# Plain fp32 matmuls on unsplit operands for the projections of one of three mixers in an encoder trunk

## The chip, the core and the metric

The kernel runs on one core of one Trainium2 chip. The metric is the device time of the program in microseconds; lower is better. A core has five engines that run side by side and meet at semaphores: PE (TensorE, the matrix multiplier; its weight loads are shown apart as PEld), DVE (VectorE), ACT (ScalarE), POOL (GpSimd) and SP (SyncE, which here issues every DMA).

## The reference

Two layers, each with an RMSNorm, one wide input projection, three mixers side by side (A: HGRN2, B: retention, C: RWKV-7), a gated merge, and an output projection. The sequence has 256 tokens, the model 1024 features. Cut to what matters:

```python
for l in range(DEPTH):                                # DEPTH = 2
    h = rmsnorm(x, norm_g[l])                         # 256 x 1024, float32
    proj = h @ w_in[l]                                # 1024 x 18688
    (a_q, a_ff, a_fb, a_i, a_g, b_q, b_k, b_v, b_g, c_s, c_g, merge) = split(proj)
    y_a = hgrn2_mixer(a_q, a_ff, a_fb, a_i, ...) * silu(a_g)
    y_b = retention_mixer(b_q, b_k, b_v, ...) * silu(b_g)
    y_c = rwkv7_mixer(c_s, ...) * silu(c_g)           # c_s: r, k, v and the codes of decay and a
    gates = sigmoid(merge)
    mixed = gates_0 * (y_a @ w_a) + gates_1 * (y_b @ w_b) + gates_2 * (y_c @ w_c)
    x = x + mixed @ w_out[l]
return rmsnorm(x, final_norm_g)
```

All of it is float32.

## The kernel before

**Weights.** The weights of a layer lie in 93 blocks of 1024 rows and 256 columns, each stored as two halves of 512 KB (`_blocks`). 17 of them feed mixer C: `codes`, and for each of eight pairs of heads `("rk", p)` (128 columns of r and 128 of k) and `("vg", p)` (128 of v and 128 of the gate). 20 feed A, 24 feed B, 12 the merge gates, 16 the branch outputs and 4 the output.

**Split products.** Every block goes through `load_w`: a half is loaded into `wr` (line 182, on SP), ACT rounds it to float32r in `wh` (line 184), and DVE subtracts the two into `wl` (line 187). The tiles `wr`, `wh` and `wl` are each taken in turn from three buffers (`RW`, through `ring`). The norm writes its transposed output h in the same way, as `h_hi` (line 253, ACT) and `h_lo` (line 254, DVE), out of the PSUM tile `n_t`. `feat_mm` then issues three float32r matmuls for each k-tile of 128 rows, wh·h_hi, wh·h_lo and wl·h_hi, 128 x 128 by 256 columns, all summed in PSUM: 24 for a half, 48 for a block (line 200; line 210 in `tok_mm`, where h is the stationary side). `proj` joins load and matmuls, and gives a PSUM tile `pj` out of two taken in turn; the profile calls it by the block's key, `p_codes`, `p_rk`, `p_vg` and so on.

**Order.** A layer first runs `c_codes`. The loop over p from -2 to 7 then runs `c_scan` of pair p, `c_prep` and `c_solve` of pair p + 2, and one pair of heads of A (p = -1 to 2) or B (p = 3 to 6) as `FILL` has it. `c_prep` projects rk and vg, shifts them along the tokens (`shift`, lines 288 to 291), and makes the chunk products (lines 393 to 399). `c_solve` sends blocks of `c_Z` to DRAM and back as `c_M` (lines 410 and 414) and inverts small triangles on DVE (lines 425 to 444). The merge (`tail`) comes after the loop. This is the order of the program; the framework orders each engine's queue itself, by a planner that runs a model of the timeline (`schedule_with_timeline_sim`), so that in the trace the matmuls of several blocks are interleaved. Each queue runs in its order, and all loads and the solve's DMAs stand in the one queue of SP.

**Plain fp32.** The small matmuls of the mixers (lines 337, 393 to 395, 486 to 534, 712, 718 and others) take float32 tiles as they are. One such matmul leaves two records in the trace.

Of the kernel before, what the change touches and what calls it, by code (L numbers as in the profile page):

```python
# [8 lines left out]
F32 = mybir.dt.float32  # L9
# [8 lines left out]
T = 256  # L18
# [9 lines left out]
RW = (3, 3, 3)  # L28
# [4 lines left out]
# columns of a layer's packed parameters  # L33
# [9 lines left out]
# columns of the shape constants  # L43
# [9 lines left out]
# of the masks that A takes, and of the rotation that B takes  # L53
# [4 lines left out]
# blocks of weights in a layer, in the order of _blocks()  # L58
BK = {}


def _blocks():
    """(key, matrix, row range start, list of (column start, width)) of each block of 1024 rows and 256 columns."""
    r = [("codes", "w_in", 0, [(11264 + 3072, 256)])]
    for p in range(8):
        r.append((("rk", p), "w_in", 0, [(11264 + 128 * p, 128), (11264 + 1024 + 128 * p, 128)]))
        r.append((("vg", p), "w_in", 0, [(11264 + 2048 + 128 * p, 128), (14592 + 128 * p, 128)]))
    for p in range(4):
        for n, o in (("aff", 1024), ("afb", 2048), ("aq", 0), ("ai", 3072), ("ag", 4096)):
            r.append(((n, p), "w_in", 0, [(o + 256 * p, 256)]))  # L70
    for p in range(4):
        r.append((("bq", p), "w_in", 0, [(5120 + 256 * p, 256)]))
        r.append((("bk", p), "w_in", 0, [(6144 + 256 * p, 256)]))
        for h in (2 * p, 2 * p + 1):
            r.append((("bv", h), "w_in", 0, [(7168 + 256 * h, 256)]))
            r.append((("bg", h), "w_in", 0, [(9216 + 256 * h, 256)]))
    for m in range(3):
        for b in range(4):
            c = 256 * b
            r.append((("mg", m, b), "w_in", 0, [(15616 + 1024 * m + c, 256)]))  # L80
            for n, w, r0 in ((("wa", "w_branch_a", 0),), (("wb0", "w_branch_b", 0), ("wb1", "w_branch_b", 1024)),
                             (("wc", "w_branch_c", 0),))[m]:
                r.append(((n, b), w, r0, [(c, 256)]))
    for b in range(4):
        r.append((("wo", b), "w_out", 0, [(256 * b, 256)]))
    return r
# [8 lines left out]
def trunk(ctx: ExitStack, tc, x, wb, pp, lora, cst, gtab, ng, out, parts="ABCT", layers=L, dbg=None):  # L95
# [10 lines left out]
    # x and what its norm takes come before the other constants  # L106
# [27 lines left out]
    def ring(pool, shape, dt, tag, n, name):  # L134
        """a tile in the next of a tag's n buffers, in turn"""
        i = turn[tag] = (turn.get(tag, -1) + 1) % n
        return pool.tile(shape, dt, tag=f"{tag}{i}", bufs=1, name=name)

    h_hi = keep.tile([128, KT, T], F32R, name="h_hi")
    h_lo = keep.tile([128, KT, T], F32R, name="h_lo")  # L140

# [1 line left out]
    DP = []  # L143
    for l in range(L):
        d = keep.tile([128, 26 + 8 + 8 + 32], F32, name=f"dp{l}")
        p = P_[l]
        mu = p[:, PO["mu"]:PO["mu"] + 52]
        # 1 - mu0 - mu1
        V.tensor_add(d[:, 0:26], mu[:, 0:26], mu[:, 26:52])
        V.tensor_scalar(d[:, 0:26], d[:, 0:26], -1.0, 1.0, op0=ALU.mult, op1=ALU.add)  # L150
        V.tensor_scalar(d[:, 26:34], p[:, PO["kk"]:PO["kk"] + 8], -1.0, None, op0=ALU.mult)
        V.tensor_scalar(d[:, 34:42], p[:, PO["ka"]:PO["ka"] + 8], -1.0, 1.0, op0=ALU.mult, op1=ALU.add)
        V.tensor_scalar(d[:, 42:74], p[:, PO["w0"]:PO["w0"] + 32], -1.0, None, op0=ALU.mult)
        DP.append(d)

    # lower bounds: softmax over the layers with its maximum, cumulated, less the first
# [13 lines left out]
    # cumsum - p[0]  # L170
# [6 lines left out]
    def load_w(l, key):  # L177
        """the parts of a block's halves"""
        W = []
        for h in range(2):  # L180
            raw = ring(wp, [128, 1024], F32, "wr", RW[0], "wr")
            nc.sync.dma_start(raw, wb[2 * (l * NBLK + BK[key]) + h])
            hi = ring(wp, [128, 1024], F32R, "wh", RW[1], "wh")
            S.copy(hi, raw)  # L184
            lo = ring(wp, [128, 1024], F32R, "wl", RW[2], "wl")
            n = WS[h]
            V.tensor_sub(lo[:, 0:n], raw[:, 0:n], hi[:, 0:n].bitcast(F32))  # L187
            if n < 1024:
                G.tensor_sub(lo[:, n:], raw[:, n:], hi[:, n:].bitcast(F32))
            W.append((hi, lo))  # L190
        return W

    def feat_mm(o, W, f, h, first=True, last=True):
        """o[feature, t] (+)= W[:, f*128:+128]^T h; half f of the block holds these columns"""
        whi, wlo = (t.rearrange("p (k c) -> p k c", c=128) for t in W[f])
        hhi, hlo = h
        n = 0
        for k in range(KT):
            for a, b in ((whi, hhi), (whi, hlo), (wlo, hhi)):
                PE.matmul(o, a[:, k], b[:, k, :], start=(first and n == 0), stop=(last and n == 3 * KT - 1))  # L200
                n += 1

    def tok_mm(o, W, t, h):
        """o[t, column] = h[:, t-tile]^T W; a half of the block holds four k-tiles"""
# [14 lines left out]

    def sigmoid_of_exp(t):  # L220
        """t = exp(-x) -> sigmoid(x), in place; Ln ends at 2^64, where sigmoid(x) = 1 / t to the last bit"""
        V.tensor_scalar(t, t, EMAX, None, op0=ALU.min)
        S.activation(t, t, AF.Ln, bias=1.0)
        S.activation(t, t, AF.Exp, scale=-1.0)
# [5 lines left out]
    def silu_from(pool, src, shape, tag, tmp, bufs=1, tb=1):  # L230
        """silu of a projection in PSUM"""
# [8 lines left out]
    def norm_T(xs, ss, gb, pool):  # L240
        """xs and the sums of its squares by token; gb: the gains, on every partition"""
# [5 lines left out]
        for t in range(2):  # L247
            for j in range(0, KT, 4):
# [5 lines left out]
                V.tensor_sub(h_lo[:, j:j + 4, 128 * t:128 * t + 128], o, hi.bitcast(F32))  # L254

# [7 lines left out]
    # ================= C: RWKV-7 =================  # L263
    pers = {}

    def c_setup(pool):
        """tiles whose blocks off the diagonal stay zero"""
# [27 lines left out]
    def c_codes(l, pool):  # L295
        o = proj(l, "codes")
        cw = shift(l, o[:, 0], 24, pool, "c_cw")
        ca = shift(l, o[:, 1], 25, pool, "c_ca")
        # tanh(x) = 2 sigmoid(2 x) - 1
# [5 lines left out]
    def c_prep(l, p, codes, pool):  # L305
        """Everything of pair p up to the chunk products, evacuated and masked."""
# [6 lines left out]
        o1 = proj(l, ("rk", p))  # L313
        r = shift(l, o1[:, 0], p, pool, "c_r", 2)
        k = shift(l, o1[:, 1], 8 + p, pool, "c_k", 2)
        o2 = proj(l, ("vg", p))
# [3 lines left out]
        # normalised kk, negated  # L320
# [8 lines left out]
        # decay and a  # L329
# [21 lines left out]
        # its ninth block holds the stacked identity  # L351
# [4 lines left out]
        # bonus: sum of r k_d r_k over both directions  # L356
# [7 lines left out]
        # k~, beta~, alpha~, r~ of each direction, and the products within its chunks  # L364
# [6 lines left out]
        for d in range(2):  # L371
            # a chunk's blocks of 64: A_rk^T, r~, A_ak, A_rb^T, beta' (first alpha~), A_ab^T, k', diag g, alpha~^T
# [30 lines left out]
    def c_solve(l, p, st, pool):  # L403
        """Inverses of the diagonal 32 x 32 blocks of I - A_ab, one block and every fourth column a partition."""
# [17 lines left out]
        # inverses of the diagonal 4 x 4 blocks, in place: entry (i, k) of block I at 132 I + 32 k + i  # L422
# [8 lines left out]
        # this block's columns  # L431
        V.tensor_mul(tp, at(m, 0, (132, 8), (1, 4), (32, 4)), cc("hot")[:, None, None, :].to_broadcast([128, 8, 4, 4]))
        V.tensor_reduce(at(w, 0, (36, 8), (1, 4)), tp, axis=AX.X, op=ALU.add)
        # then four rows at a time
# [15 lines left out]
    def c_scan(l, p, st, pool, ydst):  # L450
# [10 lines left out]
        # v of each direction, transposed  # L461
# [18 lines left out]
        # (I - A_ab)^-1 [A_ak, alpha~^T] by blocks of 32, for a direction's four chunks at a time  # L480
# [14 lines left out]
        # what a chunk makes of its v and of the state before it: mt its output, mk the state after it  # L495
# [19 lines left out]
        # the state from chunk to chunk  # L515
# [24 lines left out]
        # group norm over a head's 64 partitions  # L540
# [14 lines left out]
    # ================= A: HGRN2 =================  # L555
    def a_pair(l, p, pool, ydst):
# [6 lines left out]
        # k = (1 - lb) sigmoid(-x), f = lb + (1 - lb) sigmoid(x); the first layer's lb is p[0] - p[0] = 0  # L563
# [28 lines left out]
    def a_head(l, hd, le, kq, v, g, pool, ydst):  # L592
        # decay sums within 128 positions: forward, and backward negated
# [10 lines left out]
        def pairs(e, s):  # L604
            """K (lower forward, upper backward) and Q (lower backward, upper forward), scaled"""
# [6 lines left out]
        # between the two tiles of 128  # L612
# [30 lines left out]
        # within 8 positions, from their middle  # L643
# [16 lines left out]
        # output, its norm over the 128 partitions and the gate  # L660
# [27 lines left out]
    # ================= B: retention =================  # L688
# [52 lines left out]
    # ================= merge and output =================  # L741
# [64 lines left out]
    # ================= layers =================  # L806
# [40 lines left out]
def _consts():  # L847
# [31 lines left out]
    # [head, j, j-tile * 256 + i]  # L879
# [7 lines left out]
def _pack(inputs):  # L887
# [4 lines left out]
    for l in range(L):  # L892
        for n, (key, mat, r0, cols) in enumerate(_blocks()):
            m = np.concatenate([a[mat][l, r0:r0 + 1024, c0:c0 + w] for c0, w in cols], 1)
            if key[0] in TOK:
                # halves of four k-tiles
                m = m.reshape(2, 4, 128, 256).transpose(0, 2, 1, 3)
            else:
                # halves of 128 columns
                m = m.reshape(8, 128, 2, 128).transpose(2, 1, 0, 3)  # L900
            wb[l * NBLK + n] = m.reshape(2, 128, 1024)

    def tiles(v):
        """a vector of n * 128 values as [128, n]"""
# [40 lines left out]
```

## Time and profile before

| what | value |
|---|---|
| device time, median of 3 runs | 1821.67 us (1819.37 to 1822.58) |
| profiled execution, first to last instruction (span) | 1821.9 us |
| mean granted clock of PE | 0.965 |
| instructions | 33791 |
| weights read, 372 halves | 512 KB each |
| HBM read | 229.22 MB |

The profile gives one execution of the program; of that execution it lists the span and no other time, and the span agrees with the median of the runs to 0.2 us. Its views are a page (busy time of each engine, 40 equal slices of the span, DMA queues, the chain of waits that ended last, the costliest groups of instructions) and answers about the trace: groups by line, instructions that touch a tile, waits, the chain in order of time, and busy time by windows.

How to read it: busy time of an engine says how much of a window it worked, not whether that work was waited for; the chain says what was waited for, at one moment after the other. PE's instructions overlap in the pipeline, so the pitch from start to start is the cost of a matmul in a row of matmuls, not its duration. The blocks of C are to be found by the tiles `p_codes`, `p_rk` and `p_vg`.

### The profile page before, as it was taken

What the parts mean: (1) busy time and instruction counts of PE and PEld (TensorE: products, weight loads), DVE (VectorE), ACT (ScalarE), POOL (GpSimd) and SP (SyncE); (2) the same over time, 40 slices, a digit from 0 to 9 for tenths busy, and PEclk for the clock granted to TensorE, in tenths of its full rate; (3) what the DMA queues carried; (4) which work ended last, traced back from release to release, by engine and by line L of the source; (5) the groups of instructions that cost most, each with busy time, mean ns of one, the idle gap of its engine ahead of it and who ended that gap; (6) DMA issues with size and microseconds to landing.
All of it is one profiled execution on the core that took longest, in us unless ns stands there. A gap on an engine that the chain in (4) does not pass through costs nothing.

```text
span 1821.9 us, 33791 instructions
## 1 busy us (share of the span) xinstructions
PE 1667.6 (92%) x12960; PEld 1625.0 (89%) x12960; DVE 1415.4 (78%) x2597; ACT 1056.5 (58%) x1940; POOL 322.0 (18%) x312
## 2 busy tenths in 40 slices
PE   6888899999999999999888789988999999999997
PEld 6877899898999998999888788988889999999997
DVE  5799898998878785565657989989998787846554
ACT  5665566757465545555556556757573656456453
POOL 1122222212120200010011222223131202100100
PEclk9989999999999999999988889999999999999999
DMA  6333223324344443755533233233244444437653
GB/s 221 116 118 105 79 96 102 117 86 138 119 155 141 146 148 133 244 200 187 198 114 118 99 100 91 88 109 107 93 133 125 144 142 154 142 131 245 208 186 116
DMA packets 127873, 250.30 MB, mean 137 GB/s; under 512 B 62304, under 2 KB 66784, under 8 KB 127456
## 3 DMA queue, kind: packets, MB, share of 16 engines
q1 hardware_dynamic: 127712, 248.15, 41.6%
q8 instruction: 102, 1.67, 0.4%
q14 instruction: 59, 0.48, 0.1%
HBM read 229.22 MB, written 14.68 MB: 134 GB/s over the span
## 4 chain that ended last, share of the span: by engine, by line
PE 49%; DVE 30%; issue 7%; DMA 6%; ACT 4%; SPq 2%; POOL 0%; DVEq 0%; ACTq 0%; POOLq 0%
PE t_o L200 10%; PE p_mg L200 8%; DVE wl L187 7%; DVE c_tq L439 3%; PE p_bv L210 3%; PE p_vg L200 3%; PE p_bg L200 2%; DMA c_M<-s 2%; PE pj L210 2%; PE c_p L393 2%; DMA s<-c_Z 2%; ACT wh L184 2%; DVE c_ts L441 2%; PE p_rk L200 1%; PE c_p L395 1%
## 5 line engine op out<-in xcount | busy, mean ns | idle before, releaser
L187 DVE TENSOR_TENSOR wl<-wr,wh 128x1024 fp32r<-128x1024 f32 x372 | 475.9, 1280 | 192.3 <-ACT wh L184 190.9
L184 ACT CAST wh<-wr 128x1024 fp32r<-128x1024 f32 x372 | 388.4, 1045 | 272.7 <-PE t_o L200 56.2
L200 PE MATMUL t_o<-yh,wh 128*128 128x256 f32 x512 | 144.7, 284 | 2.8 <-ACT yh L748 2.8
L200 PE MATMUL t_o<-yl,wh 128*128 128x256 f32 x512 | 145.0, 284 | 0.5 <-DVE yl L749 0.5
L200 PE MATMUL t_o<-yh,wl 128*128 128x256 f32 x512 | 144.6, 283 | 0.0
L608 POOL TENSOR_TENSOR a_sl<-a_kq,a_e 128x256 f32<-128x256 f32 x80 | 80.9, 1015 | 230.9 <-ACT a_e L618 66.0
L200 PE MATMUL p_mg<-h_hi,wh 128*128 128x256 f32 x384 | 109.6, 285 | 0.0
L200 PE MATMUL p_mg<-h_hi,wl 128*128 128x256 f32 x384 | 109.4, 285 | 0.0
L200 PE MATMUL p_mg<-h_lo,wh 128*128 128x256 f32 x384 | 108.7, 283 | 0.0
L200 PEld LDWEIGHTS t_o<-yh,wh 128*128 128x128 f32 x512 | 97.6, 191 | 3.2 <-ACT yh L748 3.2
L200 PEld LDWEIGHTS t_o<-yl,wh 128*128 128x128 f32 x512 | 97.9, 191 | 1.0 <-DVE yl L749 0.9
L200 PEld LDWEIGHTS t_o<-yh,wl 128*128 128x128 f32 x512 | 97.9, 191 | 0.0
L393 PE MATMUL c_p<-c_Z,bbd 128*128 128x192 f32 x256 | 68.9, 357 | 29.7 <-DVE bbd L388 25.0
L439 DVE TENSOR_TENSOR c_tq<-W,c_M 128x16 f32<-128x16 f32 (+6 forms) x112 | 89.0, 795 | 1.4
L200 PE MATMUL p_vg<-h_hi,wh 128*128 128x256 f32 x256 | 78.1, 305 | 8.1 <-ACT c_k L288 4.1
L399 ACT COPY c_Z<-c_p 128x192 f32<-128x192 f32 x128 | 40.3, 318 | 74.9 <-DVE c_Z L396 73.7
L200 PE MATMUL p_bg<-h_hi,wl 128*128 128x256 f32 x256 | 75.0, 293 | 4.6 <-DVE wl L187 4.6
L210 PE MATMUL p_bv<-wh,h_hi 128*128 128x256 f32 x256 | 76.1, 297 | 1.1 <-ACT b_z L694 1.1
L210 PE MATMUL p_bv<-wl,h_hi 128*128 128x256 f32 x256 | 75.4, 295 | 1.7 <-DVE wl L187 1.7
L200 PE MATMUL p_vg<-h_lo,wh 128*128 128x256 f32 x256 | 75.8, 296 | 0.0
L200 PE MATMUL p_vg<-h_hi,wl 128*128 128x256 f32 x256 | 75.6, 295 | 0.0
L210 PE MATMUL p_bv<-wh,h_lo 128*128 128x256 f32 x256 | 74.7, 292 | 0.0
(334 smaller groups left out, 5983.3 us busy)
## 6 DMA issues: line engine op xcount, KB each, us to landing
wr<-in_wb_dram SPq DMA_DIRECT2D x372, 512.0 KB, 3.3
c_M<-s SPq DMA_DIRECT2D x64, 128.0 KB, 2.7
c_lt<-in_lora_dram SPq DMA_DIRECT2D x16, 256.0 KB, 2.7
b_sw<-b_z SPq DMA_DIRECT2D x16, 256.0 KB, 3.9
b_gt<-in_gtab_dram SPq DMA_DIRECT2D x16, 256.0 KB, 3.4
yb<-b_y SPq DMA_DIRECT2D x16, 256.0 KB, 3.0
yr<-yb SPq DMA_DIRECT2D x8, 512.0 KB, 5.0
s<-c_Z SPq DMA_DIRECT2D x128, 16.0 KB, 1.9
```

What stands on the lines that cost most here:

```text
L184: S.copy(hi, raw)
L187: V.tensor_sub(lo[:, 0:n], raw[:, 0:n], hi[:, 0:n].bitcast(F32))
L200: PE.matmul(o, a[:, k], b[:, k, :], start=(first and n == 0), stop=(last and n == 3 * KT - 1))
L210: PE.matmul(o, a[:, k, t * 128:(t + 1) * 128], b, start=(n == 0), stop=(n == 3 * KT - 1))
L393: PE.matmul(o[:, 2:5], bbd[:, c], z[:, c, 1:8:3], start=True, stop=True)
L395: PE.matmul(o[:, 0:6:5], kbd[:, c], z[:, c, 1:8:6], start=True, stop=True)
L399: S.copy(z[:, c, 4:9:2], o[:, 4:7])
L439: V.tensor_mul(tp, W[:, 0:n, None, 0:j].to_broadcast([128, n, 4, j]), M[:, 0:j, j:j + 4].rearrange("p j i -> p i j")[:, None].to_broadcast ...
L441: V.tensor_reduce(sm, tp, axis=AX.X, op=ALU.add)
L608: G.tensor_mul(s5[:, :, :, 0], k5[:, 0:2, :, 0], e5[:, :, :, 0])
```

## The change

The 17 blocks of C are no longer split. A new function `proj_whole` loads each half into `wr` and issues one plain fp32 matmul for each k-tile, straight from `wr` and from `h_f`, a third copy of h in float32 that the norm writes on ACT from the same PSUM tile: 8 matmuls for a half, 16 for a block. `wr` has four buffers. `c_codes` and `c_prep` call `proj_whole`; A, B, the merge and the output keep the split products. The scratch space that is set aside for dynamic DMAs is cut to 1024 bytes. Comments are removed as well.

```diff
-RW = (3, 3, 3)
+RW = (4, 3, 3)
...
     h_lo = keep.tile([128, KT, T], F32R, name="h_lo")
+    h_f = keep.tile([128, KT, T], F32, name="h_f")
...
+    def proj_whole(l, key):
+
+        o = ring(ps, [128, 2, 256], F32, "pj", PB["pj"], f"p_{key if key == 'codes' else key[0]}")
+        for f in range(2):
+            raw = ring(wp, [128, 1024], F32, "wr", RW[0], "wr")
+            nc.sync.dma_start(raw, wb[2 * (l * NBLK + BK[key]) + f])
+            w = raw.rearrange("p (k c) -> p k c", c=128)
+            for k in range(KT):
+                PE.matmul(o[:, f], w[:, k], h_f[:, k], start=(k == 0), stop=(k == KT - 1))
+        return o
...
                 S.copy(hi, o)
                 V.tensor_sub(h_lo[:, j:j + 4, 128 * t:128 * t + 128], o, hi.bitcast(F32))
+                S.copy(h_f[:, j:j + 4, 128 * t:128 * t + 128], o)
...
     def c_codes(l, pool):
-        o = proj(l, "codes")
+        o = proj_whole(l, "codes")
...
-        o1 = proj(l, ("rk", p))
+        o1 = proj_whole(l, ("rk", p))
...
-        o2 = proj(l, ("vg", p))
+        o2 = proj_whole(l, ("vg", p))
...
-    nc = _bacc.Bacc("TRN2", target_bir_lowering=False, num_devices=1)
+    nc = _bacc.Bacc("TRN2", target_bir_lowering=False, num_devices=1, dynamic_dma_scratch_size=1024)
```

## The prediction

> **What bounds the kernel now.** I read the head of the page first, then a table of busy time by stretches, cut where the PSUM tiles of the projections first and last appear, then the chain of waits stretch by stretch.
>
> ```profile
> span 1821.9 us, 33791 instructions
> PE 1667.6 (92%) x12960; PEld 1625.0 (89%) x12960; DVE 1415.4 (78%) x2597; ACT 1056.5 (58%) x1940; POOL 322.0 (18%) x312
> 0.00:52.00 52.00, 38.03 (x274) 36.00 (x275) 30.31 (x61) 30.93 (x55) 6.39 (x14) 1.00 0.57 203
> 52.00:410.00 358.00, 317.48 (x2435) 308.06 (x2435) 323.94 (x664) 222.11 (x448) 90.11 (x88) 0.95 0.33 103
> 410.00:695.00 285.00, 271.71 (x2088) 263.69 (x2087) 229.16 (x423) 163.29 (x311) 48.88 (x43) 0.98 0.45 141
> 695.00:905.00 210.00, 204.19 (x1689) 202.40 (x1687) 121.91 (x147) 113.36 (x157) 15.53 (x13) 1.00 0.56 191
> 905.00:955.00 50.00, 41.30 (x289) 39.25 (x290) 28.06 (x43) 26.91 (x53) 6.96 (x12) 0.86 0.40 140
> 955.00:1320.00 365.00, 320.73 (x2399) 310.94 (x2398) 326.50 (x685) 225.05 (x449) 91.35 (x87) 0.93 0.32 101
> 1320.00:1605.00 285.00, 270.36 (x2112) 262.51 (x2111) 233.26 (x431) 163.72 (x312) 47.23 (x43) 0.99 0.45 140
> ```
>
> The columns of a stretch are its window and length, the busy us of PE, PEld, DVE, ACT and POOL with their counts, the granted clock, the DMA share and GB/s. Each layer has four parts: a start (0 to 52, 905 to 955), a stretch with mixers C and A (52 to 410, 955 to 1320; the "A stretch"), one with C and B (410 to 695, 1320 to 1605; the "B stretch"), and the merge. In the A stretch DVE is busy 324 of 358 us and ACT 222; in the B stretch PE leads and DVE has 20% free. PE's busy time includes overlapping pipeline ends, so its real load is read from pitches:
>
> ```profile
> 769.47 11.52 PE t_o L200 x96
> 497.81 1.73 PE b_o L718 x8
> L187 DVE TENSOR_TENSOR wl<-wr,wh 128x1024 fp32r<-128x1024 f32 x372 | 475.9, 1280 | 192.3 <-ACT wh L184 190.9
> L184 ACT CAST wh<-wr 128x1024 fp32r<-128x1024 f32 x372 | 388.4, 1045 | 272.7 <-PE t_o L200 56.2
> ```
>
> The first two rows are of the chain: 96 float32r matmuls of 256 columns take 11.52 us, 120 ns each. Line 718 issues four plain fp32 matmuls of 256 columns; the trace holds eight records of them in 1.73 us. So one plain fp32 matmul is two records of 216 ns, 432 ns in all, and one split product, three float32r matmuls, is 360 ns. At 120 ns a record, the 2088 records of 410 to 695 fill 251 of 285 us, and more, since some are dearer fp32 ones; the 2435 of 52 to 410 fill 292 of 358. PE is near its limit in the B stretch and has up to a fifth free in the A stretch.
>
> ```profile
> by line: DVE wl L187 9.9%; issue 9.6%; DVE c_tq L439 4.8%; PE c_p L393 3.2%; DMA c_M<-s 2.9%; PE p_vg L200 2.5%; PE p_ai L210 2.5%; PE p_afb L200 2.4%; DVE a_sl L609 2.1%; DVE c_ts L441 2.1%; DMA s<-c_Z 2.1%; DVE a_e L631 2.0%; PE c_p L394
> by line: PE p_bv L210 10.4%; DVE wl L187 8.4%; issue 7.8%; PE p_bg L200 6.8%; PE p_bk L200 6.0%; PE p_bq L200 4.1%; DVE c_tq L439 3.4%; DMA c_M<-s 3.2%; DMA s<-c_Z 2.7%; PE b_o L718 2.4%; DVE c_ts L441 2.2%; PE c_p L393 2.2%; PE p_vg L200 2
> by line: issue 12.5%; DVE wl L187 7.2%; DVE c_tq L439 3.5%; PE p_vg L200 3.3%; PE p_afb L200 3.3%; PE c_p L393 3.1%; PE p_ag L200 3.0%; DVE a_sl L609 2.6%; DVE a_e L632 2.5%; DVE a_e L631 2.5%; DMA c_M<-s 2.4%; DVE c_ts L441 2.0%; DMA s<-c_
> by line: issue 9.1%; DVE wl L187 8.6%; PE p_bv L210 7.9%; PE p_bg L200 7.5%; DVE c_tq L439 4.9%; DMA c_M<-s 3.5%; DMA s<-c_Z 2.8%; DVE c_ts L441 2.5%; PE c_p L393 2.5%; PE b_o L718 2.5%; PE p_vg L200 2.1%; ACT wh L184 1.8%; DVE c_tq L442 1.
> by line: PE p_rk L200 26.0%; DMA n_g<-in_ng_dram 18.3%; PE p_codes L200 16.1%; PE p_vg L200 13.6%; ACT wh L184 6.9%; DVE wl L187 5.6%; PE n_t L251 4.5%; ACT c_xw L340 3.3%; issue 3.2%; DVE n_xn L246 3.0%; DVE c_ep L343 2.6%; DVE c_xw L222 1
> by line: PE p_rk L200 22.8%; PE p_vg L200 16.6%; PE p_codes L200 13.1%; ACT wh L184 6.3%; PE n_t L251 6.2%; issue 5.5%; DVE wl L187 5.5%; ACT c_xw L340 2.9%; DVE n_xn L246 2.6%; DVE c_xw L222 1.4%; DVE h_lo L254 1.4%; ACT vtbd L466 1.4%; DV
> ```
>
> These are the chain's shares in the A and B stretch of layer 0, the same of layer 1, and the two starts (8 to 52, 905 to 955). The reader is to see that the weight subtraction wl (DVE) is among the dearest lines of both stretches, that B's projections on PE stand beside it in the B stretch, and that the starts run through C's own projections on PE (codes, rk, vg: 55.7% and 52.5%).
>
> **The change part by part.** It touches 17 of a layer's 93 weight blocks (codes, eight rk, eight vg), 34 blocks or 68 halves in all.
>
> *Removed.* 68 casts at 1.045 us are 71.1 us of ACT, 68 subtractions at 1.280 us are 87.0 us of DVE. *Added on PE.* A block has 16 pairs of k-tile and half; each goes from 360 to 432 ns, so a block goes from 5.76 to 6.91 us, +1.15 us, and 34 blocks cost +39.2 us. Where these fall:
>
> ```profile
> 0.00:52.00 52.00, 12.00 (x96) 11.81 (x96) 3.84 (x8) 1.89 (x4) 1.00 0.57 203
> 52.00:410.00 358.00, 27.14 (x192) 24.10 (x192) 7.57 (x16) 3.80 (x8) 0.95 0.33 103
> 410.00:695.00 285.00, 13.16 (x96) 12.03 (x96) 3.83 (x8) 1.89 (x4) 0.98 0.45 141
> 0.00:52.00 52.00, 14.63 (x12) 1.00 0.57 203
> 52.00:410.00 358.00, 71.42 (x56) 0.95 0.33 103
> 410.00:695.00 285.00, 70.08 (x56) 0.98 0.45 141
> 1320.00:1605.00 285.00, 69.95 (x55) 0.99 0.45 140
> ```
>
> The first three rows are the instructions that touch p_rk (PE first), the others those of line 187. Four rk blocks (192 records) lie in layer 0's A stretch, two in its start, two in its B stretch; vg follows rk each time. So C has 8 of the A stretch's 28 blocks (16 of 56 subtractions), 4 of the B stretch's (8 of 56), and, with codes, 5 of the start's 6 (10 of 12). Layer 1 has the same programme.
>
> *A stretches.* wl holds 9.9% of 358 and 7.2% of 365 us of the chain, 61.7 us; 16/56 of that is 17.6 us that goes. Against it stand C's projections on the chain: p_vg 2.5% and 3.3%, 21 us, and p_rk, which is below the last share shown (2.0% each, at most 14 us); I take 26 us, and a fifth more of it is +5.2. The casts are off these rows; at the 1.8% that the last B row shows, 723 us hold 13.0, and 16/56 of it, 3.7, goes. Sum -16. The bounds: if DVE alone sets the pace, 16 x 1.28 = 20.5 us a layer go at a busy share of 0.90, -45 for both; if PE alone does, 16 blocks cost +18.4. I stay near the chain's reading, because when wl goes PE, at 292 plus 9 us of streaming, and DVE, at 303, are late together.
>
> *B stretches.* wl is 8.4% and 8.6% of 285 us, 48.5 us; 8/56 of it is 6.9. p_vg's 2.0% and 2.1%, 11.7 us, cost +2.3. Sum -4.6; bounds -20 (16 subtractions of 1.28 us in the two, all on the path) and +9.2 (8 blocks of 1.15 on PE).
>
> *Starts.* C's projections are 55.7% of 44 and 52.5% of 50 us of the chain, 50.8 us; a fifth is +10.2. wl and wh together are 12.5% and 11.8%, 11.4 us, of which 10/12, 9.5, are C's. h_f adds a copy of each transpose:
>
> ```profile
> engine op xcount: duration ns min/median/max, first and last start us, forms
> 14.23 0.95 ACT wh L184
> 15.20 1.22 DVE wl L187
> ```
>
> A copy of that shape takes 586 ns, four to a layer; only the first product's last tile waits for one of them, +0.6 a layer, +1.2 (all eight in a row would be +4.7). The other two rows show what goes: a cast and a subtraction on the chain ahead of the norm's own split. Sum +2; bounds -9.5 and +15.
>
> *New waits.* PE now waits for a landing itself, with all later matmuls queued behind, and a raw buffer comes free when PE has used it, not when DVE has:
>
> ```profile
> SPq L182 <- DVE wl L187: 620.0, 196, 10.3
> wr<-in_wb_dram SPq DMA_DIRECT2D x372, 512.0 KB, 3.3
> q1 hardware_dynamic: 127712, 248.15, 41.6%
> ```
>
> SP already stands 620 us behind wl before it may reload wr, and all 41.6% of DMA traffic, the solve's s and c_M transfers too, is queued on SP behind such loads. A half occupies PE for 16 x 216 ns = 3.46 us and lands in 3.3, so four buffers keep PE fed. I cost the wait at nothing, covered by the fourth buffer; without that cover each of the 12 solves outside the starts could start up to one half later, +42 us. The other end is below nothing: a buffer that no longer waits its turn in DVE's queue may come free sooner, at most the two engine steps, 2.3 us, for the same 12, -28.
>
> *The merge* has none of the changed blocks and runs at 120 ns a record: 0. The smaller DMA scratch costs nothing, since no row shows a POOL transfer. The planner orders all queues anew; the A stretch takes 358 us in one layer and 365 in the other, so I allow 7 us a layer for order, both ways.
>
> One rule of the Trainium skill speaks against the change; the rows first:
>
> ```profile
> engine op xcount: duration ns min/median/max, first and last start us, forms
> engine op xcount: duration ns min/median/max, first and last start us, forms
> ```
>
> The first row is the weight load of a plain fp32 matmul, the second of a float32r one: median 190 and 192 ns. The Trainium skill, TensorE: Matmul & The Clock Gate, "Weight-path perf modes — Fast Weight Load (FWL) and DoubleRow", says that the fast weight load is on only where the input is not FP32. By that rule the new matmuls would load slower than the old; the trace shows no difference between the two.
>
> **The sum.** -16 - 5 + 2 is -19 us, against a profiled span of 1821.9 us: 1803 us. The median of the runs shown, 1821.67, lies 0.2 us from that span, so nothing is added around it.
>
> **The rivals.**
>
> *DVE gives all its time back.* For it: 0.90 of DVE busy in the A stretch, and ACT is relieved as well. Against it: PE's lines (c_p, p_vg, p_ai, p_afb) stand on the same chain. -45 in the A stretches, -5 and +2 elsewhere: 1774 us.
>
> *PE becomes the bound (slower).* Place: PE's in-order queue in the starts and B stretches, and in the A stretch as soon as DVE's relief is used up. Price 72 ns a product. It decides where PE's free time is below the added streaming: 4.6 us a layer in the B stretch and 5.8 in the start, where its chain share is already over half. If nothing is won on DVE, that is 2 x (4.6 + 5.8), +21: 1843 us; with the A stretches +39: 1861.
>
> *The weight load is no longer hidden.* Each of the 34 x 32 records would add its load of 190 ns, +207 us: 2029 us. Against it: line 718's records keep 216 ns with such loads among them. The Trainium skill's FWL rule would lead this way; by that rule fp32 loads should be longer here, and the trace shows none.
>
> *Gain and loss cancel,* because the subtractions that go were fillers in DVE's queue: 1822 us.
>
> **How the numbers follow.** Forecast (-19, its own range 1786 to 1815) 0.45; DVE in full 0.17; cancel 0.10; PE the bound 0.26; load exposed 0.02. Predicted 1803 us. The range takes in the DVE case and reaches into the PE case, up to its middle price: 1768 to 1845. Below lies a share of the DVE case with the earlier buffers, above the +39 case, the late solves and the exposed loads, together under 0.2. Within 0.2% (3.6 us, about what a measurement of this kernel can tell from no change): 0.10; faster 0.62; slower 0.28.
>
> **What would show it.** Right: wl and wh at x304; p_codes, p_rk and p_vg as one PE group each with twice 16 records to a block at a pitch of 216 ns; the A stretch near 350 us with DVE still around 0.9; the B stretch within 5 us of 285; the starts within 2 us. Wrong: an A stretch as long as before with PE's idle time gone (PE the bound), PE waiting for wr landings or the solve's DMAs moved back behind SP (buffers held), or p_vg records further apart than 216 ns (loads exposed).

## The result and the profile after

The changed kernel takes 1851.36 us (median of four runs, 1848.56 to 1852.92), the kernel before 1820.52 us beside it: a ratio of 1.0176, 95% interval 1.0157 to 1.0194. The forecast was 1803 us; the time lies above its range.

The head of the page and the chain's shares by engine, first of the kernel before, then after; then the groups that answer to those shown before:

```profile
PE 49%; DVE 30%; issue 7%; DMA 6%; ACT 4%; SPq 2%; POOL 0%; DVEq 0%; ACTq 0%; POOLq 0%
```

```profile
span 1850.4 us, 32408 instructions
PE 1699.3 (92%) x12416; PEld 1621.9 (88%) x12416; DVE 1351.1 (73%) x2529; ACT 998.7 (54%) x1880; POOL 292.4 (16%) x312
...
PE 47%; DVE 30%; DMA 8%; issue 5%; ACT 5%; SPq 3%; POOL 1%; DVEq 0%; ACTq 0%; POOLq 0%
```

```profile
L188 DVE TENSOR_TENSOR wl<-wr,wh 128x1024 fp32r<-128x1024 f32 x304 | 391.7, 1290 | 178.9 <-ACT wh L185 172.8
L185 ACT CAST wh<-wr 128x1024 fp32r<-128x1024 f32 x304 | 317.9, 1047 | 232.4 <-PE t_o L201 57.1
...
L229 PE MATMUL p_vg<-h_f,wr 128*128 128x256 f32 x512 | 124.9, 395 | 4.1 <-DVE s_g L248 3.5
L229 PE MATMUL p_rk<-h_f,wr 128*128 128x256 f32 x512 | 120.1, 386 | 1.2 <-ACT a_v L599 1.2
```

The change did on the engines what it says: 304 casts and as many subtractions in place of 372 of each, DVE's busy time down from 1415 to 1351 us, ACT's from 1057 to 999. The chain now spends 8% of its span on DMAs and 3% in SP's queue, 11% of 1850 us, where it was 8% of 1822. Busy time by stretch, cut at the first matmul of p_aff, p_bq and p_mg and the end of pj (columns as in the prediction):

```profile
0.00:57.00 57.00, 42.94 (x192) 37.15 (x193) 19.10 (x51) 21.66 (x45) 6.39 (x14) 1.00 0.56 194
57.00:409.00 352.00, 317.89 (x2243) 299.61 (x2241) 305.82 (x647) 210.67 (x431) 78.84 (x88) 0.96 0.33 103
409.00:713.00 304.00, 285.08 (x2097) 274.21 (x2098) 226.63 (x418) 157.55 (x311) 44.52 (x43) 0.98 0.44 135
713.00:921.00 208.00, 203.47 (x1681) 201.41 (x1680) 118.23 (x142) 109.03 (x150) 16.54 (x13) 1.00 0.57 190
921.00:970.00 49.00, 42.65 (x187) 36.78 (x188) 17.61 (x32) 17.71 (x42) 6.22 (x10) 0.90 0.41 144
970.00:1333.00 363.00, 319.40 (x2259) 299.10 (x2257) 317.09 (x678) 212.94 (x436) 79.98 (x88) 0.97 0.33 101
1333.00:1633.00 300.00, 283.60 (x2077) 271.21 (x2077) 224.11 (x417) 157.20 (x310) 44.34 (x43) 0.98 0.44 135
1633.00:1850.00 217.00, 204.31 (x1690) 202.44 (x1688) 122.55 (x148) 111.93 (x161) 15.53 (x13) 0.99 0.53 177
```

The kernel before, cut in the same way, has 52, 355, 288, 208, 49, 366, 287 and 217 us. So the starts lose 5 and 0 us, the A stretches gain 3 and 3, the B stretches lose 16 and 13, and the merge is as it was. These boundaries are soft: work of a late pair of A runs on into the B stretch, so the sum of A and B is safer than either. DVE's share of the A stretch fell only from 0.90 to 0.87 while the stretch hardly became shorter.

### The profile page after: what moved, and what is told of

It is laid out like the page before. It is cut to its first block, busy times and chain, and to the rows that moved or that the text cites. A ratio compares the mean times of both kernels' runs of the same rounds, so it can differ in the third digit from the quotient of the medians.

```text
span 1850.4 us, 32408 instructions
## 1 busy us (share of the span) xinstructions
PE 1699.3 (92%) x12416; PEld 1621.9 (88%) x12416; DVE 1351.1 (73%) x2529; ACT 998.7 (54%) x1880; POOL 292.4 (16%) x312
## 4 chain that ended last, share of the span: by engine, by line
PE 47%; DVE 30%; DMA 8%; issue 5%; ACT 5%; SPq 3%; POOL 1%; DVEq 0%; ACTq 0%; POOLq 0%
PE t_o L201 10%; PE p_mg L201 7%; DVE wl L188 5%; DVE c_tq L452 4%; PE p_bg L201 3%; DMA c_M<-s 2%; PE p_bv L211 2%; PE pj L211 2%; PE p_vg L229 2%; PE p_rk L229 2%; DVE c_ts L454 2%; DMA s<-c_Z 2%; PE p_afb L201 2%; DMA wr<-in_wb_dram 1%; PE c_p L406 1%
## 5 line engine op out<-in xcount | busy, mean ns | idle before, releaser
L188 DVE TENSOR_TENSOR wl<-wr,wh 128x1024 fp32r<-128x1024 f32 x304 | 391.7, 1290 | 178.9 <-ACT wh L185 172.8
L185 ACT CAST wh<-wr 128x1024 fp32r<-128x1024 f32 x304 | 317.9, 1047 | 232.4 <-PE t_o L201 57.1
L229 PE MATMUL p_vg<-h_f,wr 128*128 128x256 f32 x512 | 124.9, 395 | 4.1 <-DVE s_g L248 3.5
L229 PE MATMUL p_rk<-h_f,wr 128*128 128x256 f32 x512 | 120.1, 386 | 1.2 <-ACT a_v L599 1.2
L229 PEld LDWEIGHTS p_vg<-h_f,wr 128*128 128x128 f32 x512 | 99.2, 200 | 18.2 <-DVE s_g L248 4.9
L621 POOL TENSOR_TENSOR a_sl<-a_kq,a_e 128x256 f32<-128x256 f32 x80 | 68.5, 860 | 282.1 <-ACT a_e L631 90.7
L229 PEld LDWEIGHTS p_rk<-h_f,wr 128*128 128x128 f32 x512 | 96.9, 194 | 14.2 <-ACT a_v L599 1.6
L201 PE MATMUL p_bg<-h_hi,wh 128*128 128x256 f32 x256 | 74.0, 289 | 0.0
```

The costliest lines, as they stand in the source:

```text
L229: PE.matmul(o[:, f], w[:, k], h_f[:, k], start=(k == 0), stop=(k == KT - 1))
L621: G.tensor_mul(s5[:, :, :, 0], k5[:, 0:2, :, 0], e5[:, :, :, 0])
```

## The experiments

Each edit changes the planner's order of all queues. Two edits that should do nothing moved the median by 3 us (a fourth raw buffer in the kernel before) and 4 us (one buffer of c_sb less in the changed kernel), so I read nothing from less than 5 us. Two edits are a small sample, and an order that happens to be worse by more than that is not excluded. Times are medians; the kernel before, timed again beside each group of runs, lay between 1820.5 and 1822.7 us in all of them. The kernels at the old price (with and without the casts), the low price and the price in float32r, those with the raw buffer held or free, and those with another order leave out C's projections; the others compute everything.

**First theory: PE's streaming.** The 31 us lost looked like the 39.2 us of added matmul time less a little relief. The first pair takes the two sides apart: `e1_split_kept` gives the split back as work that nobody reads, `e2_old_price` gives PE its old load.

```diff
 e1, in proj_whole:
+            hi = ring(wp, [128, 1024], F32R, "wh", RW[1], "wh")
+            S.copy(hi, raw)
+            lo = ring(wp, [128, 1024], F32R, "wl", RW[2], "wl")
+            V.tensor_sub(lo, raw, hi.bitcast(F32))
 e2, in proj_whole:
-            for k in range(KT):
-                PE.matmul(o[:, f], w[:, k], h_f[:, k], start=(k == 0), stop=(k == KT - 1))
+            for n in range(23):
+                k = n % KT
+                if n == 1:
+                    PE.matmul(o[:, f, 0:128], w[:, k], h_f[:, k, 0:128], start=False, stop=False)
+                else:
+                    PE.matmul(o[:, f], h_lo[:, k, 0:128], h_hi[:, k], start=(n == 0), stop=(n == 22))
```

> The changed kernel with the casts and subtractions of C's 34 blocks put back as work whose result nobody reads: PE's new price with no relief of DVE and ACT. Theory 1 (PE's streaming price of 72 ns a product, 39 us in all, is what shows; the relief is worth little): 1851 to 1862 us, the relief worth at most 10 us. The forecast's reading (the relief is worth its share of the chain, about 38 us): 1885 us or more. Theory 2 (the order of the queues, or raw buffers held by PE, costs the time): no clear prediction, within 10 us of the changed kernel either way.

> The changed kernel at the old price on PE: for each half of C's blocks 22 float32r matmuls of 256 columns on h's own parts and one plain fp32 matmul of 128 columns that reads the raw half, 22 x 120 + 2 x 108 = 2.86 us in place of 8 x 432 = 3.46 us (before: 24 x 120 = 2.88 us). C's projections are left out of the computation; loads, raw buffers, h_f and the missing split are as in the changed kernel. Theory 1: 1810 to 1820 us, that is the time before less the little that the relief is worth. The forecast's reading of the relief: about 1782 us. Theory 2 (order, or buffers held until PE has used them): it stays near 1845 to 1855 us.

Measured: 1874.70 us (ratio 1.0286, 1.0257 to 1.0315) and 1801.12 us (0.9887, 0.9858 to 0.9916). So the relief is worth 23 us at the new price (1874.7 less 1851.4), more than the theory's 10 us and less than the forecast's 38, and a kernel with the relief and PE's old load is 21 us faster than before. The changed kernel takes 50 us more than that one, and its matmuls stream 41 us longer (68 halves x 0.6 us).

**Where the relief sits.** The casts alone were put back into the run at the old price, and PE's load was cut further:

```diff
 e8 = e2, and:
+            hi = ring(wp, [128, 1024], F32R, "wh", RW[1], "wh")
+            S.copy(hi, raw)
 e9 = e2 with
-            for n in range(23):
+            for n in range(11):
```

> The run at the old price on PE, with the casts of C's 68 halves put back on ACT (read by nobody), the subtractions still gone: relief of DVE alone. If the relief is DVE's: 1801 us, as without the casts. If it is ACT's: 1820 us. If both share it: between.

> The run at the old price on PE with 10 float32r matmuls a half in place of 22: 1.42 us a half, 2.04 us less than the changed kernel, 139 us in all, and 98 us less than the run at the old price; C's projections are left out again. If PE's stream sets the pace everywhere: 1801 - 98 = 1703 us. If DVE or the dependent chain of C and A takes over as soon as PE is relieved: 1770 us or more.

Measured: 1804.54 us and 1760.31 us. The relief is DVE's: ACT's 71 us of casts cost 3, less than can be told from nothing here. And 98 us less on PE bring only 41, so neither expectation of the second run holds in full; PE is one bound among others.

**By stretch.** Plain fp32 for some pairs only (the others, and codes, split as before):

```diff
-        o1 = proj_whole(l, ("rk", p))
+        pj_c = proj_whole if p in (2, 3, 4, 5) else proj      # e3; (6, 7) in e4; (0, 1) and codes in e5
+        o1 = pj_c(l, ("rk", p))
...
-        o2 = proj_whole(l, ("vg", p))
+        o2 = pj_c(l, ("vg", p))
```

> Plain fp32 only for pairs 2 to 5, the 16 blocks of the two A stretches; codes and the other pairs split as before; h_f and four raw buffers kept. If DVE's relief counts where DVE is busiest, as the forecast had it: 1805 us (-16). Stretch by stretch from the changed kernel's trace (A stretches -5, nothing elsewhere): 1816 us. Theory 1 with PE's price carried on to wherever PE is next full: 16 of 34 blocks, +18 less a few us of relief, 1830 to 1837 us.

> Plain fp32 only for pairs 6 and 7, the 8 blocks of the two B stretches. If these blocks themselves cause the 29 us that the B stretches lose in the changed kernel: 1845 to 1850 us. Theory 1 (each block costs its own 1.15 us of PE and the rest of the loss is work that came late from the stretch ahead): +9, 1828 to 1832 us.

> Plain fp32 only for codes and pairs 0 and 1, the 10 blocks of the two starts; the rest split as before; h_f and four raw buffers kept. Theory 1 (PE's added streaming is paid in full, relief in part): 10 x 1.15 = +11.5 us less the gain of a start without splits (8 us in layer 0 and 3 in layer 1 by the run at the old price): 1822 to 1828 us. If the start lost in the two runs that kept its split (8 us in layer 0) comes from h_f and the fourth buffer and stays: 1830 us.

Measured: 1831.73, 1834.10 and 1826.88 us: +10, +12 and +4. The first and the third lie in the ranges that the streaming theory gave, the second 2 us above its range, so these runs did not yet speak against it. No part of the change wins by itself, and the losses do not follow the number of blocks (16, 8 and 10). In the first two layer 0's start is 59 and 60 us where it was 52, though its blocks are split as before; h_f was the suspect.

**h_f.** The copies alone in the kernel before, and then the A stretches' run with h_f made by POOL from h's parts:

```diff
 e7, in the kernel before:
+                S.copy(h_f[:, j:j + 4, 128 * t:128 * t + 128], o)
 e11 = e3, and:
-                S.copy(h_f[:, j:j + 4, 128 * t:128 * t + 128], o)
+                G.tensor_add(h_f[:, j:j + 4, 128 * t:128 * t + 128], hi.bitcast(F32),
+                             h_lo[:, j:j + 4, 128 * t:128 * t + 128].bitcast(F32))
```

> The kernel before with the eight copies to h_f added, which nobody reads, three raw buffers, and the small DMA scratch. If h_f's copies stand on the path of the start (ACT's casts of h wait behind them): +4 to +8 us, 1826 to 1830 us, most of it in layer 0's start. If the fourth raw buffer made the loss there: 1822 us. The forecast had +1.2 us for the copies.

> Plain fp32 for pairs 2 to 5 alone, as in the run of the A stretches, but h_f is made by POOL as the sum of h's two parts, so that ACT has no copy among its casts of h. If the copies on ACT cost what they cost by themselves (about 11 us): 1818 to 1823 us, and layer 0's start is back near 52 us. If they do not: 1831 us.

Measured: 1833.52 us (ratio 1.0058, 1.0036 to 1.0080) and 1824.30 us (1.0013, 1.0001 to 1.0026). ACT's queue in the start of the run with the copies, and the third cast of h in the kernel before (start and length in us):

```profile
13.09 0.59 ACT L254 CAST h_hi<-n_t 128x512 fp32r<-128x512 f32 x1 [0.27 <-PE n_t L252]
13.77 0.59 ACT L256 COPY h_f<-n_t 128x512 f32<-128x512 f32 x1
14.25 1.05 ACT L185 CAST wh<-wr 128x1024 fp32r<-128x1024 f32 x1
...
15.33 0.58 ACT L256 COPY h_f<-n_t 128x512 f32<-128x512 f32 x1
15.79 1.06 ACT L185 CAST wh<-wr 128x1024 fp32r<-128x1024 f32 x1
16.74 0.60 ACT L254 CAST h_hi<-n_t 128x512 fp32r<-128x512 f32 x1
```

```profile
15.49 0.59 ACT L253 CAST h_hi<-n_t 128x512 fp32r<-128x512 f32 x1 [0.19 <-PE n_t L251]
```

Two copies now stand among the casts of h and of weights, and the third cast of h starts at 16.74 us, where it started at 15.49 before. The copies cost 11 us in the kernel before. In its trace the span is 16 us longer than the kernel before's, and 8 of these lie in the two starts; the rest lies in the stretches behind them and was not explained. In the run of the A stretches POOL's copy gives 7 us back, and its layer 0 starts A at 54 us in place of 59. In the changed kernel no cast of C's weights stands between the copies, and its starts lost 5 us in all.

**Streaming, tested by itself.** The run at the old price, with the new price paid in float32r matmuls:

```diff
 e10 = e2 with
-            for n in range(23):
+            for n in range(28):
```

> The run at the old price on PE with 27 float32r matmuls a half in place of 22: 27 x 120 + 2 x 108 ns = 3.46 us, the changed kernel's price, paid in float32r matmuls; C's projections are left out again. If the price is PE's streaming time alone: as the changed kernel, 1846 to 1856 us. If plain fp32 matmuls cost more than they stream (or are misjudged by the planner): 1801 + 41 = 1842 us or less.

Measured: 1797.65 us (0.9873, 0.9850 to 0.9896). This is where the first theory fell: with the raw buffer free early, 41 us more of streaming on PE cost nothing (1801 to 1798). The trace shows that PE did spend the time: from the start of each record of C's blocks to the start of PE's next record, waits included, it is 239 us in the run at the old price, 274 here and 273 in the changed kernel. So the 54 us between this run and the changed kernel (1851.4 less 1797.7) are not the time that PE streams. Two things still differed: the raw buffer was free after the second matmul of a half, and no matmul but that one was plain fp32.

**Buffers held, and plain fp32.** The two were crossed:

```diff
 e13 = e10 with the raw half read late:
-                if n == 1:
+                if n == 26:
 e14 = the changed kernel with the raw half read early:
-                PE.matmul(o[:, f], w[:, k], h_f[:, k], start=(k == 0), stop=(k == KT - 1))
+                PE.matmul(o[:, f], w[:, k] if k == 1 else h_lo[:, k, 0:128].bitcast(F32), h_f[:, k], start=(k == 0), stop=(k == KT - 1))
```

> The run that pays the changed kernel's price in float32r matmuls, with the one matmul that reads the raw half put last but one in place of second, so that PE holds the raw buffer through the half as the changed kernel does; C's projections are left out again. If the held buffers are what costs the changed kernel its 53 us against that run: about 1850 us. If not: about 1798 us.

> The changed kernel with its 16 plain fp32 matmuls a block, but only the second of each half reads the raw weights; the others take a fixed plain fp32 operand, so the raw buffer is free after 0.86 us in place of 3.46. C's projections are left out. If the held buffers cost the 53 us: about 1798 us. If plain fp32 itself does (its duration, or an order of the queues planned with another price for it): about 1850 us.

| | raw buffer free early | raw buffer held through the half |
|---|---|---|
| float32r, 3.46 us a half | 1797.65 | 1816.19 |
| plain fp32, 3.46 us a half | 1834.49 | 1851.36 |

Each run lies between its two expectations: both matter. Holding costs 17 to 19 us, plain fp32 35 to 37 at equal streaming. For the second, PE's time in C's blocks, counted as above, is 274 us in both runs with a free buffer, so the matmuls themselves are not longer; the loss is spread over the starts (+1 and +3 us), the A stretches (+10 and +5) and the B stretches (+6 and +8). The free-buffer pair was then repeated with the framework's other planner:

```diff
-    with _tile.TileContext(nc, schedule_with_timeline_sim=True) as tc:
+    with _tile.TileContext(nc, schedule_with_timeline_sim=False) as tc:
```

> The run that pays the changed kernel's price in float32r matmuls (1798 us), its queues ordered by the framework without the model of the timeline. It serves with the next one: the pair shows what plain fp32 costs under another order. By itself: 1850 to 2000 us.

> The run with plain fp32 and the raw buffer freed early (1834 us), its queues ordered without the model of the timeline. If plain fp32 costs the hardware 36 us beyond its streaming: 36 us, within 10, above the run with float32r under the same order. If the loss came from the order that the timeline's model made for plain fp32: within 10 us of that run.

Measured: 1881.06 and 1878.21 us. Under this order plain fp32 costs nothing beyond its streaming. This order is itself some 80 us slower than the planned one with float32r, and a cost off PE could hide in it. With PE's equal time in C's blocks it points to the order that is planned around plain fp32 matmuls, not to the matmuls, as the source of the 36 us; that the orders differ can be counted (C's matmuls are followed by another tile's 140 times in the float32r run and 94 times in plain fp32), but that the order makes the loss is argued and not shown, and what it does wrong was not found.

**One more buffer.** If held raw buffers are the trouble, a fifth must help. For its room c_sb gives up one of four buffers, and a control makes that edit alone; the fourth was also tried in the kernel before.

```diff
 e17, in the changed kernel:
-LA, ZB, YB, SB, CT = 2, 4, 3, 4, 3
+LA, ZB, YB, SB, CT = 2, 4, 3, 3, 3
-RW = (4, 3, 3)
+RW = (5, 3, 3)
 e18: the first of the two alone
 e6, in the kernel before: RW = (4, 3, 3) and the small DMA scratch
```

> The changed kernel with five raw buffers in place of four (and three buffers of c_sb in place of four, for the room). If the held buffers cost the 17 us that the two pairs of runs show: 1835 to 1845 us. If a buffer more does not loosen them: 1851 us.

> The changed kernel with three buffers of c_sb in place of four and its four raw buffers: the control for the run with five. If the fifth raw buffer made that run 30 us faster than the changed kernel: 1848 to 1856 us here. If the smaller c_sb (or the new order that any such edit brings) did: about 1822 us.

> The kernel before with four raw buffers and the small DMA scratch alone. Split weights free their raw buffer early, so a fourth should be worth little: 1818 to 1824 us. If SP's 620 us of waiting for raw buffers counted: 1810 us or less.

| kernel | median us | ratio to before, 95% interval |
|---|---|---|
| five raw buffers (e17) | 1821.60 | 0.9998 (0.9982 to 1.0014) |
| control, four (e18) | 1855.46 | 1.0179 (1.0155 to 1.0203) |
| kernel before with four (e6) | 1825.65 | 1.0014 (0.9997 to 1.0032) |

The fifth buffer gives back 34 us against its control, more than the 17 to 19 that the crossed runs had put down to holding. The two costs of that table may not be independent, or part of the gain may be a better order; these runs do not tell the two apart. Stretch by stretch, cut as above, the kernel with five buffers gains 22 us in the A stretches against the kernel before, loses 14 in the B stretches and 5 in the starts.

SP's waits at the loads of split blocks (us in total, times, longest) and ACT's idle time before a cast until its raw half has landed, first of the changed kernel, then of the run with five buffers:

```profile
SPq L183 <- DVE wl L188: 471.9, 154, 11.3
SPq L183 <- PE p_rk L229: 90.2, 20, 10.5
SPq L183 <- PE p_vg L229: 27.6, 11, 4.6
...
ACT wh L185 <- DMA wr<-in_wb_dram: 55.2, 25, 5.5
```

```profile
SPq L183 <- DVE wl L188: 430.3, 146, 9.8
SPq L183 <- PE p_rk L229: 52.1, 17, 5.6
SPq L183 <- PE p_vg L229: 33.0, 17, 4.6
...
ACT wh L185 <- DMA wr<-in_wb_dram: 40.5, 22, 7.3
```

With four buffers SP, about to load a half of A, B or the merge, stands 90 us until PE has done with an rk half, up to 10.5 us at a time; with five it is 52, up to 5.6. The control has 91.4, up to 10.8. All rows of SP's two load lines that name C's matmuls come to 161 us in the changed kernel and 164 in the control, and to 123 with five buffers. In the crossed runs they are 207 held against 136 free in float32r, and 122 free in plain fp32. This is the wait that goes with holding.

ACT's wait for raw halves is no such sign:

```profile
ACT wh L184 <- DMA wr<-in_wb_dram: 14.9, 8, 2.9
```

That is the kernel before. The control has 56.8, but the float32r run with a free buffer, at 1798 us, has 47.8 as well, and the plain fp32 run with a free buffer 56.3. On the chain the landing of raw halves is largest in one place: in the changed kernel's B stretch of layer 1 it holds 5.1%, and the same row of the kernel before, in the prediction, ends at shares of 1.8% without it:

```profile
by line: DVE wl L188 7.1%; PE p_bv L211 6.6%; PE p_bg L201 6.3%; issue 5.9%; DMA wr<-in_wb_dram 5.1%; DVE c_tq L452 4.9%; PE p_bq L201 2.8%; DMA c_M<-s 2.4%; DVE c_ts L454 2.2%; DVE c_Z L395 2.1%; ACT wh L185 2.0%; PE c_p L406 2.0%; DVE c_t
```

In layer 0, whose B stretch lost 16 us, the row goes down to shares under 2% without it, so this landing does not account for the loss there. In the crossed float32r pair it holds 3.5% of each B stretch where the buffer is held, and at most 2.1% where it is free.

**A version for both.** To relieve DVE with nothing new on PE, POOL took a quarter of every second half's subtraction in the kernel before (`WS = (1024, 768)`).

> The kernel before, with the last quarter of every second half's subtraction given to POOL: DVE is relieved of 186 x 0.3 = 56 us with no new work on PE. If DVE's relief is worth what it is worth at the old price (about a third of its size): 1805 to 1812 us. If the wait for POOL eats it: 1822 us or more.

Measured: 1849.98 us (1.0156, 1.0136 to 1.0175), 29 us slower. The groups of this run that differ:

```profile
L187 DVE TENSOR_TENSOR wl<-wr,wh 128x1024 fp32r<-128x1024 f32 (+1 forms) x372 | 435.4, 1171 | 202.8 <-ACT wh L184 199.4
...
L189 POOL TENSOR_TENSOR wl<-wr,wh 128x256 fp32r<-128x256 f32 x186 | 232.0, 1247 | 721.0 <-ACT wh L184 681.8
```

The relief that was meant to be tested hardly came about. POOL takes 1247 ns for its quarter, about as long as DVE takes for a whole half (1280); DVE's subtractions fall by 40 us, not by 56, and DVE's busy time as a whole only from 1415 to 1411 us, with others of its instructions longer than before. SP's waits change hands without growing:

```profile
SPq L182 <- DVE wl L187: 845.5, 264, 13.9
...
SPq L182 <- POOL wl L189: 57.0, 97, 1.9
```

The first row was 620 us before, but all rows of this load line together come to 1089 us, and to 1102 before. So this run does not say what a relief of DVE is worth without new work on PE, and what makes it 29 us slower was not found. None of the kernels that compute everything beat the kernel before.

## Why the prediction was wrong, point by point

- **The step that failed** is "I cost the wait at nothing, covered by the fourth buffer". The argument there was that a half occupies PE for 3.46 us and lands in 3.3, so that four buffers keep PE fed. It looked at C's blocks alone, as if PE ran them one after the other. PE was in fact fed: none of its idle time before a matmul of line 229 is put down to a landing. But the ring is shared and taken in turn: a buffer of C is held until PE, in its own order, has run the block's last matmul on it, and SP, in whose one queue all loads stand, waits for that before it loads the next half of A, B or the merge (161 us in all, up to 10.5 at a time). Measured, the wait that was set to nothing costs 17 to 19 us by the crossed runs and 34 by the fifth buffer. How SP's standing turns into those microseconds of the span was not followed further.
- **The bound of +42 us** was given for the case without the cover, and 34 is near it by luck. It counted 12 solves that start a half late, and the trace shows no clear sign of that: POOL's wait for the solve's transfers (c_M) is 119.6 us where it was 128.6, DVE's 29.9 where it was 19.3.
- **The order** of the queues was allowed 7 us a layer, both ways. If the 36 us that come with plain fp32 at equal streaming are the planner's order, as argued above, this allowance, 14 us for both layers, was too small as well.
- **The relief** was forecast as DVE's, and it is, but its size was too large. In the sum, what goes with wl and wh came to 38 us (17.6 + 3.7 for the A stretches, 7 for B, 9.5 for the starts); measured, 23 at the new price, and 21 net in the run at the old price.
- **The price on PE** was right as a price: the chain of the changed kernel has 32 records of p_vg in 6.91 us, 216 ns each, and 6.91 us a block.

```profile
33.62 6.91 PE p_vg L229 x32
```

  What it costs was charged at 18 us of the chain (5.2 + 2.3 + 10.2). By the run that pays it in float32r it costs nothing on the whole; in the starts it is paid (49 and 41 us in the run at the old price, 55 and 47 there) and the stretches absorb it.
- **h_f** was charged at 1.2 us, from the cast of the same shape:

```profile
L253 ACT CAST h_hi<-n_t x8: 586/586/589, 12.8 to 912.9; 128x512 fp32r<-128x512 f32 x8
```

  By itself it costs 11 in the kernel before. In the changed kernel the starts lost 5 us together against a forecast of +2.
- **The A stretches** were to gain 16 and gained 6; the **B stretches** were to gain 5 and lost 29. With five buffers the A stretches gain 22, so there the forecast lacked only the buffer; the B stretches still lose 14.
- **The rivals.** The measured time lies inside the one named PE the bound (1843 to 1861 us), but not for its reason: the same streaming in float32r brings 1798. For the weight load, the rows of a plain fp32 and of a float32r matmul in the kernel before, and of the new matmuls, are:

```profile
L337 PEld LDWEIGHTS c_lo<-c_cw,c_lt x64: 186/190/338, 42.3 to 1496.4; 128*128 128x128 f32 x64
L200 PEld LDWEIGHTS t_o<-yh,wh x512: 186/192/192, 717.9 to 1787.9; 128*128 128x128 f32 x171
...
L229 PEld LDWEIGHTS p_rk<-h_f,wr x512: 186/190/337, 21.1 to 1504.4; 128*128 128x128 f32 x171
```

  The new load takes 190 ns at the median, as long as the old, and is hidden, as the pitch of 216 ns shows. The rule that was weighed from the Trainium skill (TensorE: Matmul & The Clock Gate, "Weight-path perf modes — Fast Weight Load (FWL) and DoubleRow") had no part in the time that a run here shows. The rival that came true, held buffers, stood in the prediction as the upper end of a cost, and had no chance of its own, only a part in the less than 0.2 left outside the range.

Left open: where the 36 us with plain fp32 come from, why the B stretches lose 14 us even with five buffers, and why the run with five buffers, at 1821.6 us, does not come down to the 1798 of the run in float32r with a free buffer. Nothing was tried on these, and the kernel before was not run with five.

## What to carry to other kernels

When an operand is used straight from its load buffer instead of from a copy, count the time until the last reader on the slowest queue has passed it, for the whole ring and everything loaded in turn behind it, and not the load's time against its own use; test it by adding one buffer, with a control for the room that it takes. An engine's added time and the price of a new operation can be told apart by paying the same time in the old operation. A bound of +42 us that is worked out and then set to nothing should be a rival with a chance of its own. And where a planner orders the queues anew with every edit, an experiment needs a control that replans and does nothing else.

## What the runs showed of the hardware that was not expected

A plain fp32 matmul of 256 columns occupies PE for 432 ns (two records of 216) and the three float32r ones of a split product for 360 (three of 120), with weight loads of 190 and 192 ns hidden under both: the split is the cheaper of the two on PE. POOL took 1247 ns to subtract 128x256 float32 elements, where DVE took 1280 for 128x1024. And 41 us of added matmul time did not show in the time of the kernel at all (1801.1 to 1797.7 us), while 98 us less brought only 41.
